# Three reorderings in a two-layer attention trunk: which queue issues the opening loads, when the memory rows are squared, when the block couples start

## The chip, the cores and the metric

The kernel runs on one core of a Trainium2 chip. The core has a matrix engine (TensorE, here PE, with its weight loader PEld), a vector engine (VectorE, DVE), a scalar engine (ScalarE, ACT), GpSimd (POOL) and SyncE (SP), which here only issues DMAs. Each engine works through its own instructions in order, and waits on semaphores for the others. The metric is the time of one execution in microseconds on the device.

## The reference, cut to what matters

Two layers over 256 tokens of width 1024, in fp32. Layer 0 has three head groups side by side: native sparse attention (compressed blocks, selected blocks, window), block attention (8 heads, which with 256 tokens and blocks of 256 is plain causal attention) and cross attention into 256 memory tokens. Layer 1 has retention and memory attention.

```python
def even_layer(x, mem_n, ...):
    h = rms_norm(x, norm_g)
    (nq, nkc, nvc, nks, nvs, nkw, nvw, ng, nz, mq, mk, mv, mz, eq, ez) = _split(h @ w_in, EVEN_SPLITS)
    kc = nsa_compress(rot(nkc), pe_k, w1_k, w2_k)
    vc = nsa_compress(heads(nvc), pe_v, w1_v, w2_v)
    gates = jax.nn.sigmoid(ng + gate_b).reshape(Bsz, T, NSA_BRANCHES, NSA_HEADS)
    a_out = nsa_attention(rot(nq), kc, vc, rot(nks), heads(nvs), rot(nkw), heads(nvw), gates)
    b_out = moba_attention(rot(mq), rot(mk), heads(mv))
    m_out = memory_attention(heads(eq), mem_n, w_mem_kv)
    y = jnp.concatenate([a_out * jax.nn.silu(nz), b_out * jax.nn.silu(mz),
                         m_out * jax.nn.silu(ez)], axis=-1) @ w_out
    return x + y
```

`mem_n` is the memory after an RMS norm over its rows, which needs the sum of squares of each row. `h` is the RMS norm of x, with the norm's weights folded into x's transposed tiles and the row scale applied later.

## The kernel before, in words

**Three products for one.** Each fp32 operand is split into a rounded part and a remainder (`whi` and `wlo` for weights, `xh` and `xl` for x), and `mm3` (lines 245 to 247) computes high times high, high times low and low times high. So each weight tile of 128 x 1024 (512 KB, a *unit* of two k-tiles by 512 columns) takes a load into a `raw` buffer, a cast on ScalarE into `whi` (`fetch`, line 166) and a subtraction on VectorE into `wlo` (`finish`, line 174). `unit()` hands out the next pair and fetches one that is used two units later. There are six `raw` buffers and four each of `whi` and `wlo`.

**The opening.** Before the stages, lines 380 to 398 issue the first loads by hand: x transposed (`xT`, eight k-tiles), the norm weights `g0`, and the weights of the first projection in halves and quarters. ScalarE issues x's k-tiles 0 and 1, SP the rest in order. PE runs a few warm-up matmuls (line 400), and then the first projection, k-tile by k-tile (lines 402 to 410): ScalarE multiplies x's k-tile by the norm weights into `xh` (`gain_cast`), VectorE makes `xl` (`gain_low`), and the k-tile's weights are split (`split`, lines 144 and 146). The weights of k-tile 0 are cast on VectorE, the others on ScalarE.

**Turns.** All that follows in layer 0 is a sequence of *stages*, each the projection of one group of columns, eight turns long: `compress`, `sparse_queries`, `sparse_gates`, `block_keys`, `block_queries`, `block_values`, `block_gates`, `memory_queries`, `memory_keys`, then the output projection `first_out`. A stage yields after each group of matmuls (twelve of 256 columns, or six of 512), and at each yield `drive` runs one `turn()`: it counts `slot[0]` up and advances every running *task* by one step. Tasks are generators; a step issues instructions on several engines and yields. The instructions go to each engine in exactly the order in which this program issues them (`manual_schedule`). Tasks in `first` (the attention couples) go before those in `active` (all else). The table `AT` names turns that tasks wait for with `until`.

**Couples.** `couple` computes attention for two pairs of heads, one step a turn: take four PSUM banks and issue the scores (step 0), maxima of the first pair (1), maxima of the second and exponentials of the first (2), exponentials of the second and softmax scaling of the first (3), scaling of the second (4), transposes of the first (5), copies of it and transposes of the second (6), copies (7), the product with the values in bank "o" (8); then `gated` multiplies with the gate path, casts, and subtracts (9 to 11), and the bank "o" is given back in step 9. Step 8 puts the couple's name into `made`, and a couple in `waiting` whose needs are all in `made` starts in that same turn. Four sparse couples, two block couples and the memory attention follow one another like this. `take(n, tags)` waits until n of the named banks are free; a bank given back in a turn is free in the next. `crowded` keeps "tr" from the couples, since the output projection accumulates there.

**Memory rows.** `memory_scale` loads the memory's rows (`memtok`), squares each of the two tiles on ScalarE with a row sum (`row_scale`, line 418), computes the reciprocal root on VectorE, and broadcasts it with two small matmuls into `rbm`, which `memory_keys` needs.

**Compression.** `compressed` waits for turn `AT["cmp"]`, rotates the keys (line 336 by way of `rotate`), copies the values (line 732), transposes three turns later (lines 739 and 740), adds the position weights from turn `AT["blk"]` on (line 759), and runs the compression matmuls in turn `AT["hid"]`, then the compressed scores.

Of the kernel before, what the change touches and what calls it, by code (L numbers as in the profile page):

```python
# [30 lines left out]
BANKS = {"pj": 3, "tr": 1, "t": 1, "s0": 1, "s1": 1, "o": 1}  # L31
FREE = ("s0", "s1", "t", "tr", "o")
NEG = -1e30
AT = {"rows": 4, "rows1": 4, "spread": 12, "ret": 75, "nsa": 12, "cmp": 15, "blk": 18, "hid": 24}
MAGIC = 12582912.0
PI_LO = 3.1415925
BASE = 16512 + 32 + 416 + 32
# [24 lines left out]
def trunk(  # L62
# [19 lines left out]
    nc = tc.nc  # L82
# [20 lines left out]
    def load(t, src):  # L103
        nc.sync.dma_start(t, src)
        return t
# [80 lines left out]
    waiting, first, active, made, slot, free = deque(), [], [], set(), [0], {}  # L186
# [16 lines left out]
    def take(n=1, tags=FREE[:4]):  # L203

        while sum(is_free(tag) for tag in tags) < n:
            yield
        got = [tag for tag in tags if is_free(tag)][:n]
        for tag in got:
            free[tag] = 1 << 30
        return got  # L210
# [6 lines left out]
    def drive(stage, every=1):  # L217

        for i, _ in enumerate(stage):
            if i % every == 0:  # L220
                turn()
# [6 lines left out]
    def pause(n):  # L228

        for _ in range(n):  # L230
            yield
# [6 lines left out]
    def making(task, *names):  # L238

        yield from task  # L240
        made.update(names)
# [121 lines left out]
    xraw, wraw = [], []  # L363
# [13 lines left out]
    order = ExitStack()  # L377
    order.enter_context(tc.manual_schedule(engines=MANUAL))
    g0 = vect[:, V_G0 : V_G0 + 8]
    load(wraw[0][:, 0:512], w512[2][:, 0:512])  # L380
    for kt in range(2):
        nc.scalar.dma_start(xraw[0][:, kt : kt + 1], xT[:, kt : kt + 1])
    load(g0, vec[:, V_G0 : V_G0 + 8])
    load(wraw[0][:, 512:1024], w512[2][:, 512:1024])
    for q in range(1, 4):
# [87 lines left out]
    def tables1():  # L473

        yield from until(AT["ret"])
        rows = load(cs[:, 64:].bitcast(I32), posrow.to_broadcast([P, T]))
# [4 lines left out]
    def norms():  # L481

        yield from until(AT["rows"])
        yield from row_scale(xrow, rstd0, D, AT["rows1"])
# [69 lines left out]
                else:  # L554
                    V.tensor_scalar(p[:, hh, a], p[:, hh, a], sm[:, hh, tok : tok + 1], None, op0=ALU.mult)  # L555

    def couple(jobs, causal, products, close, name, need=None):

        spans, cols, blocks = (SPAN, 384, range(3)) if causal else (HALF, 512, (0, 2, 1, 3))
        tags = yield from take(4, FREE)  # L560
        ss, todo = [], []
        for i, (q, k, gate) in enumerate(jobs):
            ss.append([bank(tag) for tag in tags[2 * i : 2 * i + 2]])
            for tok, a in enumerate(spans):
                for hh in range(2):
                    rows = slice(64 * hh, 64 * hh + 64)
                    todo.append((ss[i][hh][:, a], q[rows, tok * P : (tok + 1) * P], k[rows, : a.stop - a.start], True, True))
        side_by_side(todo)
        yield
        ps, ms, ns, pts = [[None] * 2 for _ in range(4)]  # L570

        def maxima(i):

            ps[i] = tl("p", [P, 2, 512], 2)
            ms[i] = tl("mx", [P, 2, 2], 4)
            ns[i] = tl("sm", [P, 2, 2], 4)
            for hh in range(2):
                if causal:
                    for tok, a in enumerate(spans):
                        V.tensor_tensor_reduce(ps[i][:, hh, a], ss[i][hh][:, a],  # L580
                                               cpak[:, C_CAUSAL + a.start : C_CAUSAL + a.stop], -1.0, 3e38,
                                               ALU.add, ALU.min, ms[i][:, hh, tok : tok + 1])
                else:
                    V.tensor_reduce(ms[i][:, hh], ss[i][hh].rearrange("p (a k) -> p a k", a=2), AX.X, ALU.max, negate=True)
            if causal:
                give(*tags[2 * i : 2 * i + 2])

        def exponentials(i):

            for hh in range(2):  # L590
                for tok, a in enumerate(spans):
                    src = ps[i][:, hh, a] if causal else ss[i][hh][:, a]
                    S.activation(ps[i][:, hh, a], src, AF.Exp, bias=ms[i][:, hh, tok : tok + 1],  # L593
                                 scale=-1.0 if causal else 1.0, accum_out=ns[i][:, hh, tok : tok + 1])
            if not causal:
                give(*tags[2 * i : 2 * i + 2])

        def scale(i):

            softmax_scale(ps[i], ns[i], spans, jobs[i][2], 0 if jobs[i][2] is None and causal else 3)  # L600

        def turned(i):

            held = yield from take(2, FREE)
            return [(tag, transposes([ps[i][:, hh, b * P : (b + 1) * P] for b in blocks], tag)) for hh, tag in enumerate(held)]

        def copies(i, held):

            pts[i] = tl("pt", [P, 2, 512], 2)
            for hh, (tag, b) in enumerate(held):  # L610
                got = S.copy(pts[i][:, hh, :cols], b)
                give(tag)
            return got

        maxima(0)
        yield
        maxima(1)
        exponentials(0)
        yield
        while need is not None and "gates" not in made:  # L620
            yield
        exponentials(1)
        scale(0)
        yield
        scale(1)
        yield
        first = yield from turned(0)
        yield
        copies(0, first)
        second = yield from turned(1)  # L630
        yield
        got = copies(1, second)
        yield
        while need is not None and need not in made:
            yield
        tag, = yield from take(1, ("o",))
        o = bank(tag)
        side_by_side(products(o, pts), got)
        made.add(name)
        yield  # L640
        yield from close(o)
# [6 lines left out]
    def gated(o, szT, y, kts):  # L648

        n = (kts.stop - kts.start) * T  # L650
        yf = tl("tmp2", [P, 512], 3)[:, :n].rearrange("p (k t) -> p k t", t=T)
        V.tensor_tensor(yf, o[:, :n].rearrange("p (k t) -> p k t", t=T), szT[:, kts], ALU.mult)
        give("o")
        yield
        S.copy(y[:, 0, kts], yf)
        yield
        V.tensor_tensor(y[:, 1, kts], yf, y[:, 0, kts].bitcast(F32), ALU.subtract)
# [185 lines left out]
    def memory_queries():  # L843
        nonlocal eqT, szm
        ps_e = yield from project_turned((xh, xl))
        eqT = tl("s2", [P, 2, T], NS)
        szm = tl("s2", [P, 2, T], NS)

        def post():
            scaled(ps_e[0], rb0, 0.125, eqT)  # L850
            yield from gate_path(ps_e[1:], rb0, szm)

        active.append(making(post(), "eqT", "szm"))
# [14 lines left out]
    def memory_scale():  # L868
        nonlocal rstdm, rbm
        mrow = [load(tl("raw", [P, 1024], NRAW), memtok[:, tok]) for tok in range(2)]  # L870
        rstdm = tl("rstdm", [P, 2])
        yield
        yield from row_scale(mrow, rstdm, D)
        yield
        rbm = tl("rbm", [P, T])
        tag, = yield from take()
        b = bank(tag)
        for tok in range(2):
            PE.matmul(b[:, tok * P : (tok + 1) * P], rstdm[:, tok : tok + 1].to_broadcast([P, P]), ident, start=True, stop=True)
        yield  # L880
        V.tensor_copy(rbm, b[:, :T])
        give(tag)

    def memory_keys():
        nonlocal memk, memv
        assert {"mh", "rbm"} <= made
        ps = yield from project_mem((mh, ml))
        memk = tl("s2", [P, 2, T], NS)
        memv = tl("s2", [P, 2, T], NS)

        def post():
            mem_keys(ps, rstdm, rbm, memk, memv)
            yield

        active.append(making(post(), "memk"))
# [31 lines left out]
    def block_couple(c):  # L927
        nonlocal yb
        if c == 0:
            yb = tl("y", [P, 2, 4, T], 2, F32R)  # L930

        def products(o, pts):
            todo = []
            for i in range(2):
                todo += causal_products(o[:, i * T : i * T + T], pts[i],
                                        lambda hh, kt: mvt[:, kt, (4 * c + 2 * i + hh) * 64 : (4 * c + 2 * i + hh) * 64 + 64],
                                        True, True)
            return todo

        yield from couple([(mq[:, 2 * c + i], mk[:, 2 * c + i], None) for i in range(2)], True, products,  # L940
                          lambda o: making(gated(o, szb, yb, slice(2 * c, 2 * c + 2)), f"Yb{c}"), f"yb{c}")

    def memory_keys1():
        nonlocal k1, v1m
# [31 lines left out]
    drive(block_values())  # L976
    active.append(making(memory_scale(), "rbm"))
    drive(block_gates())
    waiting.extend(({"mq", "mk", "mvt", "szb", f"yb{c - 1}" if c else "yn3"}, block_couple(c)) for c in range(2))
    drive(memory_queries())  # L980
    crowded = True
    drive(memory_keys())


    def part(acc, tok, c0, n, y, k, wh, wl, start, stop):
# [321 lines left out]
```

## Time and profile before

| | us |
|---|---|
| median of 3 runs | 427.76 |
| lowest, highest | 427.15, 428.31 |
| the profiled execution | 427.74 |
| its span, first to last instruction | 425.9 |
| mean granted TensorE clock | 0.999 |
| DMA: 74.23 MB over the span | mean 174 GB/s |

A row of the timeline gives start and length in us, engine, line, operation, and output and inputs by tile name; in brackets the idle time of the engine before it and what ended that. Neighbouring instructions of a kind are merged, with their count behind an x. PE's lengths are modelled and overlap, so the distance from start to start tells more than the length does.

### The profile page before, as it was taken

The page shows a single profiled execution, that of the slowest core. Times are in us where ns is not written, and L with a number is a line of the kernel's source. Part 1 is how long each engine was busy: PE and PEld are TensorE (multiplying, and loading weights), DVE is VectorE, ACT ScalarE, POOL GpSimd, SP SyncE. Part 2 cuts the span into 40 slices and gives each one's busy share as a digit, 9 for nine tenths or more (in the row PEclk, how much of TensorE's full clock was granted, in tenths as well). Part 3 has the DMA queues.
Part 4 walks back from the last instruction along what each step waited for, and adds up shares of the span by engine and source line. Part 5 has one row for each costly group of instructions (what it writes and reads, how often), then busy time and mean ns, then how long its engine had stood idle before and what let it go on. Part 6 is the DMA issues. An engine that isn't in the chain of part 4 may idle for free.

```text
span 425.9 us, 7020 instructions
## 1 busy us (share of the span) xinstructions
PE 417.7 (98%) x2620; PEld 361.4 (85%) x2620; DVE 305.7 (72%) x675; ACT 245.6 (58%) x453; POOL 1.9 (0%) x9
## 2 busy tenths in 40 slices
PE   8999999999999999999999999999999999999994
PEld 6889987878889887779999988889998888888884
DVE  3878996977678577588578675677887467685545
ACT  4768476777777586755456344456444445545613
POOL 1000000000000000000000000000000000000000
PEclk9999999999999999999999999999999999999999
DMA  7997545254563852536445545546444555656202
GB/s 247 334 372 254 194 136 192 67 184 160 184 191 110 287 175 97 169 128 195 157 145 168 170 167 168 196 159 198 158 158 159 184 192 175 205 170 189 80 0 99
DMA packets 22801, 74.23 MB, mean 174 GB/s; under 512 B 2928, under 2 KB 4464, under 8 KB 22768
## 3 DMA queue, kind: packets, MB, share of 16 engines
q1 hardware_dynamic: 22192, 73.14, 52.2%
q10 hardware_dynamic: 576, 0.66, 0.6%
q8 instruction: 20, 0.33, 0.3%
q14 instruction: 13, 0.11, 0.1%
HBM read 72.73 MB, written 1.05 MB: 173 GB/s over the span
## 4 chain that ended last, share of the span: by engine, by line
PE 92%; DVE 3%; DMA 3%; ACT 1%; issue 0%; SPq 0%; DVEq 0%; ACTq 0%
PE pj L245 23%; PE pj L247 22%; PE pj L246 22%; PE o L116 3%; PE s L409 2%; PE s L324 2%; PE s L116 2%; PE t L324 1%; DMA raw<-in_w 1%; PE tr L245 1%; PE tr L247 1%; PE tr L246 1%; DMA raw<-in_memtok 1%; PE t L116 1%; PE s L246 1%; PE s L247 1%
## 5 line engine op out<-in xcount | busy, mean ns | idle before, releaser
L174 DVE TENSOR_TENSOR wlo<-raw,whi 128x1024 fp32r<-128x1024 f32 (+1 forms) x118 | 142.1, 1207 | 61.8 <-ACT whi L166 59.7
L166 ACT CAST whi<-raw 128x1024 fp32r<-128x1024 f32 (+1 forms) x118 | 121.7, 1036 | 88.4 <-PE pj L247 38.0
L245 PE MATMUL pj<-whi,big 128*128 128x512 f32 (+2 forms) x256 | 97.3, 383 | 0.0
L246 PE MATMUL pj<-wlo,big 128*128 128x512 f32 (+2 forms) x256 | 96.1, 376 | 0.0
L247 PE MATMUL pj<-whi,big 128*128 128x512 f32 (+2 forms) x256 | 95.8, 374 | 0.0
L245 PE MATMUL pj<-big,whi 128*128 128x256 f32 x256 | 73.6, 287 | 0.0
L247 PE MATMUL pj<-big,wlo 128*128 128x256 f32 x256 | 72.6, 284 | 0.0
L246 PE MATMUL pj<-big,whi 128*128 128x256 f32 x256 | 72.5, 283 | 0.0
L245 PEld LDWEIGHTS pj<-whi,big 128*128 128x128 f32 x256 | 48.2, 188 | 9.3 <-issue 1.5
L247 PEld LDWEIGHTS pj<-whi,big 128*128 128x128 f32 x256 | 48.2, 188 | 8.7
L246 PEld LDWEIGHTS pj<-wlo,big 128*128 128x128 f32 x256 | 48.3, 189 | 8.1 <-DVE wlo L174 0.4
L245 PEld LDWEIGHTS pj<-big,whi 128*128 128x128 f32 x256 | 49.0, 191 | 1.9 <-issue 1.8
L246 PEld LDWEIGHTS pj<-big,whi 128*128 128x128 f32 x256 | 49.0, 192 | 0.1
L247 PEld LDWEIGHTS pj<-big,wlo 128*128 128x128 f32 x256 | 49.0, 191 | 0.0
L593 ACT ACTIVATE p<-p,mx 128x128 f32<-128x128 f32 (+1 forms) x48 | 21.2, 443 | 5.3 <-DVE mx L580 5.3
L245 PE MATMUL pj<-whi,y 128*128 128x512 f32 x42 | 16.9, 407 | 0.0
L247 PE MATMUL pj<-whi,y 128*128 128x512 f32 x42 | 16.4, 390 | 0.0
L246 PE MATMUL pj<-wlo,y 128*128 128x512 f32 x42 | 16.3, 391 | 0.0
L555 DVE TENSOR_SCALAR p<-p,sm 128x256 f32<-128x256 f32 (+1 forms) x48 | 12.7, 322 | 0.6
L343 ACT ACTIVATE big<-raw,vec 128x256 fp32r<-128x256 f32 x16 | 7.7, 505 | 5.2 <-DMA vec<-in_vec 2.5
L553 ACT ACTIVATE p<-p,sm 128x256 f32<-128x256 f32 (+1 forms) x16 | 7.6, 484 | 4.9 <-DVE sm L549 4.0
L580 DVE CUSTOM_DVE_ANT_0 p<-s,cst 128x128 f32<-128x128 f32 (+1 forms) x24 | 7.1, 355 | 4.4 <-PE s L116 4.3
(349 smaller groups left out, 644.5 us busy)
## 6 DMA issues: line engine op xcount, KB each, us to landing
raw<-in_w SPq DMA_DIRECT2D x90, 512.0 KB, 3.9
raw<-in_wout SPq DMA_DIRECT2D x28, 512.0 KB, 4.1
v<-in_xtok SPq DMA_DIRECT2D x4, 512.0 KB, 6.4
raw<-in_w SPq DMA_DIRECT2D x4, 280.0 KB, 5.3
raw<-in_w SPq DMA_DIRECT2D x4, 256.0 KB, 6.2
v<-in_w SPq DMA_DIRECT2D x2, 512.0 KB, 7.5
raw<-in_memT SPq DMA_DIRECT2D x2, 512.0 KB, 4.2
raw<-in_memtok SPq DMA_DIRECT2D x2, 512.0 KB, 4.9
```

Source lines behind the costliest of these rows:

```text
L116: ins = PE.matmul(out, lhs, rhs, start=start, stop=stop)
L166: S.copy(hi, raw)
L174: V.tensor_tensor(lo, raw, hi.bitcast(F32), ALU.subtract)
L245: PE.matmul(ps, lh, rh, start=start, stop=False, skip_group_check=shared)
L246: PE.matmul(ps, lh, rl, start=False, stop=False, skip_group_check=shared)
L247: return PE.matmul(ps, ll, rh, start=False, stop=stop, skip_group_check=shared)
L324: PE.transpose(b[:, i * P : (i + 1) * P], a, ident)
L343: S.activation(hi[:, kt], raw[:, kt - k0], AF.Copy, scale=g[:, kt : kt + 1])
L409: PE.matmul(ps_k[tok], x[:, kt, tok * P : (tok + 1) * P], w, start=kt == 0 and i == 0, stop=kt == KT - 1 and i == 2)
L553: S.activation(p[:, hh, a], p[:, hh, a], AF.Copy, scale=sm[:, hh, tok : tok + 1])
L555: V.tensor_scalar(p[:, hh, a], p[:, hh, a], sm[:, hh, tok : tok + 1], None, op0=ALU.mult)
L593: S.activation(ps[i][:, hh, a], src, AF.Exp, bias=ms[i][:, hh, tok : tok + 1], scale=-1.0 if causal else 1.0, accum_out=ns[i][:, hh, tok : ...
```

## The change

It makes five small edits and adds and removes no computation. The first load on SP is x's k-tile 0, in front of the norm weights; the first half of the weights and x's k-tile 1 are issued by ScalarE. `cmp` and `hid` move by one turn. `memory_scale` waits one turn more before the squares and two more before the broadcast. The block couples no longer need `szb`, the gate path's tile (it is read in step 9), and the second one takes its banks in the order "tr", "s0", "s1", "t". `crowded` is set after `memory_keys` instead of before.

```diff
-AT = {"rows": 4, "rows1": 4, "spread": 12, "ret": 75, "nsa": 12, "cmp": 15, "blk": 18, "hid": 24}
+AT = {"rows": 4, "rows1": 4, "spread": 12, "ret": 75, "nsa": 12, "cmp": 14, "blk": 18, "hid": 23}
...
-    load(wraw[0][:, 0:512], w512[2][:, 0:512])
-    for kt in range(2):
-        nc.scalar.dma_start(xraw[0][:, kt : kt + 1], xT[:, kt : kt + 1])
+    nc.scalar.dma_start(wraw[0][:, 0:512], w512[2][:, 0:512])
+    nc.scalar.dma_start(xraw[0][:, 1:2], xT[:, 1:2])
+    load(xraw[0][:, 0:1], xT[:, 0:1])
     load(g0, vec[:, V_G0 : V_G0 + 8])
...
-    def couple(jobs, causal, products, close, name, need=None):
+    def couple(jobs, causal, products, close, name, need=None, banks=FREE):
...
-        tags = yield from take(4, FREE)
+        tags = yield from take(4, banks)
...
-        yield
+        yield from pause(2)
         yield from row_scale(mrow, rstdm, D)
-        yield
+        yield from pause(3)
...
-                          lambda o: making(gated(o, szb, yb, slice(2 * c, 2 * c + 2)), f"Yb{c}"), f"yb{c}")
+                          lambda o: making(gated(o, szb, yb, slice(2 * c, 2 * c + 2)), f"Yb{c}"), f"yb{c}",
+                          banks=("tr", "s0", "s1", "t") if c else FREE)
...
-    waiting.extend(({"mq", "mk", "mvt", "szb", f"yb{c - 1}" if c else "yn3"}, block_couple(c)) for c in range(2))
+    waiting.extend(({"mq", "mk", "mvt", f"yb{c - 1}" if c else "yn3"}, block_couple(c)) for c in range(2))
     drive(memory_queries())
+    drive(memory_keys())
     crowded = True
-    drive(memory_keys())
```

## The prediction, made before the changed kernel was run

> **What bounds the kernel now.** I read the page first, then the waits of PE and of its weight loader, then the timelines of PE, ScalarE and VectorE wherever PE waited.
>
> ```profile
> span 425.9 us, 7020 instructions
> PE 417.7 (98%) x2620; PEld 361.4 (85%) x2620; DVE 305.7 (72%) x675; ACT 245.6 (58%) x453; POOL 1.9 (0%) x9
> PE s L324 <- DVE p L555: 1.2, 1, 1.2
> ```
>
> TensorE is the bound: matmuls stand back to back for 98% of the span. No instruction is added or removed by this change (loads swap queues, tasks swap turns), so all it can win is time in which PE waits. After the opening there are only two such places: 1.2 us for the scaled softmax `p` of a couple, and a small one for `ym`, shown further down. I add PE's lead-in, and the cost of PE switching between full matmuls and the side-by-side 64-row ones.
>
> The larger wait, on PE, with the same transposes of a later couple as a yardstick:
>
> ```profile
> 110.22 0.28 PE L245 MATMUL pj<-big,whi 128*128 128x256 f32 x1
> 111.66 0.28 PE L245 MATMUL pj<-big,whi 128*128 128x256 f32 x1
> 115.86 0.28 PE L247 MATMUL pj<-big,wlo 128*128 128x256 f32 x1
> 117.29 1.03 PE L324 MATMUL s<-cst,p 128*128 128x128 f32 x6 [1.16 <-DVE p L555]
> 136.11 0.82 PE L324 MATMUL s<-cst,p 128*128 128x128 f32 x6
> ```
>
> A turn's group of twelve matmuls takes 111.66 - 110.22 = 1.44 us, 0.12 each. So PE was free at 115.86 + 0.12 = 115.98 and began at 117.29: **1.31 us** lost. The six transposes then took 1.03 instead of 0.82, as half of them still waited: **0.21 us**.
>
> Why was `p` late?
>
> ```profile
> 103.60 0.49 ACT L611 COPY pt<-o 128x384 f32<-128x384 f32 x1
> 107.71 1.06 ACT L418 ACTIVATE raw<-raw 128x1024 f32<-128x1024 f32 x1 [3.62 <-DMA raw<-in_memtok]
> 108.77 1.03 ACT L166 CAST whi<-raw 128x1024 fp32r<-128x1024 f32 x1
> 109.70 1.05 ACT L418 ACTIVATE raw<-raw 128x1024 f32<-128x1024 f32 x1
> 110.76 1.03 ACT L166 CAST whi<-raw 128x1024 fp32r<-128x1024 f32 x1
> 112.00 0.40 ACT L593 ACTIVATE p<-p,mx 128x128 f32<-128x128 f32 x1
> 115.10 0.50 ACT L593 ACTIVATE p<-p,mx 128x256 f32<-128x256 f32 x1
> 117.01 0.51 ACT L553 ACTIVATE p<-p,sm 128x256 f32<-128x256 f32 x1 [1.32 <-DVE sm L549]
> 109.83 1.23 DVE L174 TENSOR_TENSOR wlo<-raw,whi 128x1024 fp32r<-128x1024 f32 x1 [5.49 <-ACT whi L166]
> 116.95 0.74 DVE L555 TENSOR_SCALAR p<-p,sm 128x128 f32<-128x128 f32 x3
> ```
>
> ScalarE runs in order. The first memory square (L418) stood ahead of a weight cast (L166) and waited 3.62 us for its rows; the cast could have gone at 104.1. VectorE's `wlo` needs that cast, so VectorE idled 5.49 us, then worked off its queue and reached the scaling of `p` at 116.95.
>
> **The change part by part.**
>
> *Memory squares.* Turn N is the one at 105.29. Rows are still asked for at turn N-2; the squares move from N-1 and N to N and N+1. The cast of N's unit is issued before turn N, so it now runs at 104.1 to 105.1 and its `wlo` until 106.4, 4.7 us sooner than 111.1. Queued behind the waiting square are now the second square, the next cast and the exponentials. Bounding pessimistically, I let the second square start no earlier than its 109.70: cast at 110.76 and exponentials from 112.00 to 115.6 as before. What changes is VectorE: output product, both maxima and the first rsqrt step fit before 112.9, the next `wlo` before 114.1, the first scaling after the fourth exponential (113.8) by 115.2. ScalarE's share of it (L553, 0.51) follows the last exponential: 116.2. PE's first three transposes need only VectorE's share (115.2, against 115.98); the fourth needs 116.2 at 116.3. Cover: 0.8 and 0.1 us; with the second square at its data, 0.5. I take the whole **1.52 us**. Bounds: 0 and 1.52. The later broadcast of the memory scale finds its banks taken at turn N+8 and goes at N+10, its copy at N+11, still before the memory keys (N+14).
>
> *Block scores.* Without `szb` the first block couple starts in the turn of the last sparse product instead of one later. With "tr" in place of "o" (which the product holds) the second starts in the first one's product turn instead of two later; moving `crowded` is what lets it have "tr". So couples run 1, 3 and 3 turns earlier (block 0, block 1, memory). PE's work is the same, but products and scores now stand together:
>
> ```profile
> 105.29 1.52 PE L116 MATMUL o<-pt,s 128*64 128x256 f32 x16
> 107.17 0.93 PE L116 MATMUL s<-s,v 64*128 64x128 f32 x8
> 123.79 1.52 PE L116 MATMUL o<-pt,s 128*64 128x256 f32 x16
> 125.67 0.38 PE L245 MATMUL pj<-big,whi 128*128 128x256 f32 x1
> 127.30 0.93 PE L116 MATMUL s<-v,v 64*128 64x128 f32 x8
> ```
>
> Joined, product to scores is 107.17 - 105.29 = 1.88 us, the same as product to full matmul when apart (125.67 - 123.79). But the group standing between the two takes 127.30 - 125.67 = 1.63 instead of 1.44. Joining saves that 0.19 once per block couple: **0.38 us** (bounds 0 and 0.4).
>
> *Memory attention, three turns earlier,* leaves the out-projection's last group of `ym` nothing to wait for:
>
> ```profile
> 183.84 0.40 PE L246 MATMUL pj<-wlo,ym 128*128 128x512 f32 x1
> 184.23 0.50 PE L247 MATMUL pj<-whi,ym 128*128 128x512 f32 x1
> 184.56 0.40 PE L245 MATMUL pj<-whi,ym 128*128 128x512 f32 x1
> 184.80 0.40 PE L246 MATMUL pj<-wlo,ym 128*128 128x512 f32 x1
> ```
>
> The first two stand 0.39 apart, the last two 0.24; the third matmul needs the `ym` remainder that VectorE has just written. I take 0.39 - 0.23 = **0.16 us** (bounds 0 and 0.16).
>
> *`cmp` 15 to 14, `hid` 24 to 23.* PE does not wait here now, so nothing can be won directly; the question is cover.
>
> ```profile
> 33.55 1.06 ACT L166 CAST whi<-raw 128x1024 fp32r<-128x1024 f32 x1
> 35.73 0.37 ACT L732 ACTIVATE tmp<-t,rstd 128x128 f32<-128x128 f32 x1 [0.50 <-DVE gates L728]
> 35.61 1.21 DVE L174 TENSOR_TENSOR wlo<-raw,whi 128x1024 fp32r<-128x1024 f32 x1
> 38.10 0.69 DVE L336 TENSOR_TENSOR rot_a<-pj,ctq 128x512 f32<-128x512 f32 x1 [1.27 <-PE o L739]
> ```
>
> The compress copies (L732) now stand ahead of a weight cast on ScalarE: it starts at 36.1 instead of 33.55, its `wlo` ends at 38.4 instead of 36.8. L739 is PE's work of turn 18 and ended VectorE's wait at 38.10; this unit is used in turn 19, a group of 1.44 later, about 39.5, so some 1.1 us of cover stay. In exchange the 1.27 us that VectorE waited for L739 go, as those transposes come a turn earlier; VectorE ends within 0.3 us of where it was. The compressed scores stay in their turn: the first sparse couple holds the banks. Price 0; if the cover were gone, up to the 2.55 us by which the cast moves.
>
> *The opening.* SP's first issue becomes x's k-tile 0 (128 KB) instead of half a weight tile (256 KB); that half goes out on ScalarE's queue ahead of k-tile 1. The norm weights keep their place behind it.
>
> ```profile
> 5.65 1.04 ACT L343 ACTIVATE big<-raw,vec 128x256 fp32r<-128x256 f32 x2 [2.50 <-DMA vec<-in_vec]
> 7.50 0.62 ACT L144 CAST whi<-raw 128x512 fp32r<-128x512 f32 x1 [0.80 <-DMA raw<-in_w]
> 8.43 0.51 ACT L343 ACTIVATE big<-raw,vec 128x256 fp32r<-128x256 f32 x1 [0.31 <-DMA raw<-in_xT]
> 9.06 0.62 ACT L144 CAST whi<-raw 128x512 fp32r<-128x512 f32 x1
> 8.17 1.21 PE L409 MATMUL s<-whi,big 128*128 128x512 f32 x4
> 9.74 1.20 PE L409 MATMUL s<-whi,big 128*128 128x512 f32 x4
> ```
>
> The first cast waits for the norm weights (5.65), and they may land some tenths sooner. But PE's second and third k-tiles start at 8.17 and 9.74, right behind the casts of weights that land near 7.5 and 9.0. Before the second half lands, the same 772 KB must have come over both queues as before. What is won on k-tile 0 therefore turns into a longer wait at 8.17: price **0**. From outside: 256 KB of the stream land in about 8.43 - 7.50 = 0.93 us, so the 128 KB that change queues are worth 0.47 us either way. The Trainium skill ("DMA: Bandwidth & Descriptors", section "Issuing engines are not separate DMA queues") says that DMAs issued by different engines run on the same 16 DMA engines and interleave, and that issuing from several saves only issue time. By that rule the opening is worth nothing; by queues of their own it would be worth the 0.47. No row here decides it.
>
> **Sum.** 1.52 + 0.38 + 0.16 + 0 = 2.06 us off the profiled execution's 427.74 (span 425.9 and 1.84 around it): 425.7. That execution is 0.02 from the median of the runs, 427.76.
>
> **The rivals.**
> - *Queues of their own:* everything behind SP's first load lands 0.47 sooner: 425.2. For it: only the second half's place in SP's queue; against it: the later waits (8.43) show a stream that is full.
> - *More sharing:* ScalarE's queue carries 128 KB more ahead of the second half, which lands 0.47 later: 426.1.
> - *The square still blocks:* moved by one turn it holds the next cast and the exponentials instead, the cover of 0.1 us is gone, and the stall stays: 425.7 + 1.52 = 427.2. For it: exponentials from 112.00 as before in my pessimistic bound; against it: VectorE's 5.49 idle us are gone.
> - *VectorE becomes the bound (slower):* block 1's maxima and scaling now fall into the turns of block 0's output steps.
>
> ```profile
> L580 DVE CUSTOM_DVE_ANT_0 p<-s,cst 128x128 f32<-128x128 f32 (+1 forms) x24 | 7.1, 355 | 4.4 <-PE s L116 4.3
> L555 DVE TENSOR_SCALAR p<-p,sm 128x256 f32<-128x256 f32 (+1 forms) x48 | 12.7, 322 | 0.6
> 102.00:104.00 2.00, 2.00 (x19) 2.00 (x18) 2.00 (x3) 2.00 (x5) 0.00 (x0) 1.00 0.71 188
> ```
>
> Eight maxima at 0.355 and six scalings at 0.322 are 4.8 us. With two and a half `wlo` of 1.23 and about 1 us of output steps that is an estimated 8.9 us in five turns, which PE fills for 5 x 1.44 + 1.88 + about 1.5 = 10.6. It decides if VectorE enters them more than 1.7 us behind; each further us then delays a `wlo` and PE. With all 4.8 exposed: 430.5. Against it: sparse couples stack the same way, and at 102 to 104 VectorE is full (2.00) while PE is too.
>
> **How the numbers follow.** Forecast 0.55 (425.2 to 426.4), own queues 0.12, more sharing 0.11, square still blocks 0.15, VectorE bound 0.07. About 0.3%, here 1.28 us, is what a measurement can tell from no change: the edges are 426.5 and 429.0. Faster: 0.51 of the forecast's 0.55, 0.12 and 0.08 of the sharing case make 0.71. Same: the remaining 0.07 and the 0.15 make 0.22. Slower: 0.07. The range reaches from the own-queue case with a little for error, 425.0, to the blocked square, 427.3, and leaves out the slower case and tails.
>
> **What would show it.** Right: no PE wait for L555 near 114 to 118; a weight cast on ScalarE between the L611 copies and the first L418; scores directly behind the product, without `pj` between, for both block couples; `ym` matmuls evenly 0.23 apart; k-tile 1 still near 8.2. Wrong: a PE wait for `wlo` or `whi` near 39 to 50 (cover at `cmp` gone) or between the block couples; k-tile 1 at 7.7 or 8.6; a wait of the exponentials that still ends at 117.

## The result, and the profile after

| | before | after |
|---|---|---|
| median in us | 427.76 (427.00 to 428.85, 5 runs) | 425.46 (424.62 to 425.79, 5 runs) |
| ratio to before | | 0.9942, 95% interval 0.9923 to 0.9962 |
| span of the profiled execution | 425.9 | 423.9 |
| the changed kernel timed once more, later | 427.97 (10 runs) | 425.90 (6 runs), ratio 0.9951, 0.9936 to 0.9966 |

The change makes the kernel 2.3 us faster, 2.1 us in the second timing. The prediction was 425.7, in a range from 425.0 to 427.3. One execution of a kernel further down, e_norms, ran at a granted clock of 0.558 and took 694.15 us; it was the profiled one, and it is left out of all times and of the table of starts.

The same lines of the page as before the change (busy time, share of the span and instructions of each engine), now of the changed kernel:

```profile
span 423.9 us, 7022 instructions
PE 416.1 (98%) x2620; PEld 361.4 (85%) x2620; DVE 306.1 (72%) x675; ACT 246.0 (58%) x453; POOL 1.9 (0%) x9
```

And PE's waits in it (what it wrote, which engine and line ended the wait, then us in total, times, and the longest):

```profile
PE t L400 <- POOL kcbd L716: 1.3, 1, 1.3
PE s L409 <- ACT whi L144: 0.3, 1, 0.3
PE pj L246 <- DVE wlo L174: 0.3, 1, 0.3
```

The wait of 1.2 us for `p` has left the list. What remains is the lead-in (L400), which before had too, and two waits of 0.3 in the first 28 us, which before's profile did not have.

The place of the old stall, in the timelines of ScalarE, VectorE and PE of the changed kernel (start, length, engine, line, operation, output and inputs, and in brackets the idle time ahead with what ended it):

```profile
105.04 1.07 ACT L166 CAST whi<-raw 128x1024 fp32r<-128x1024 f32 x1
108.27 1.06 ACT L418 ACTIVATE raw<-raw 128x1024 f32<-128x1024 f32 x1 [2.17 <-DMA raw<-in_memtok]
106.14 1.23 DVE L174 TENSOR_TENSOR wlo<-raw,whi 128x1024 fp32r<-128x1024 f32 x1 [1.37 <-ACT whi L166]
114.41 0.74 DVE L555 TENSOR_SCALAR p<-p,sm 128x128 f32<-128x128 f32 x3
116.78 0.82 PE L324 MATMUL s<-cst,p 128*128 128x128 f32 x6
```

The cast stands ahead of the square now, so `wlo` follows at 106.14, where before it began at 109.83. ScalarE still waits 2.17 us for the memory's rows, and the next cast and the exponentials stand behind, but they are still in time for PE. VectorE scales `p` at 114.41 instead of 116.95, PE takes up the transposes at 116.78 without a wait, and the six take 0.82 us.

The product of the last sparse couple and the scores of the first block couple, then `ym` in the output projection, both on PE:

```profile
122.49 1.52 PE L116 MATMUL o<-pt,s 128*64 128x256 f32 x16
124.37 0.93 PE L116 MATMUL s<-v,v 64*128 64x128 f32 x8
125.88 0.39 PE L245 MATMUL pj<-big,whi 128*128 128x256 f32 x1
181.88 0.39 PE L245 MATMUL pj<-whi,ym 128*128 128x512 f32 x1
182.10 0.39 PE L246 MATMUL pj<-wlo,ym 128*128 128x512 f32 x1
182.33 0.39 PE L247 MATMUL pj<-whi,ym 128*128 128x512 f32 x1
182.56 0.39 PE L245 MATMUL pj<-whi,ym 128*128 128x512 f32 x1
```

Product to scores is 1.88 us and scores to the next projection matmul 1.51 us, each as it was before when they stood apart (127.30 to 128.81 for the latter, by the matmul that stands at 128.81 in before's timeline). Gone is the group that lay between them, at 1.63 instead of 1.44. From the first to the fourth `ym` matmul it takes 0.68 us; in before it took 184.56 - 183.50 = 1.06.

### The profile page after: what moved, and what is told of

Its sections match the earlier page's. It is cut to its first block, busy times and chain, and to the rows that moved or that the text cites. A ratio compares the mean times of both kernels' runs of the same rounds, so it can differ in the third digit from the quotient of the medians.

```text
span 423.9 us, 7022 instructions
## 1 busy us (share of the span) xinstructions
PE 416.1 (98%) x2620; PEld 361.4 (85%) x2620; DVE 306.1 (72%) x675; ACT 246.0 (58%) x453; POOL 1.9 (0%) x9
## 4 chain that ended last, share of the span: by engine, by line
PE 84%; DMA 6%; DVE 4%; ACT 3%; issue 1%; SPq 0%; DVEq 0%; ACTq 0%
PE pj L245 22%; PE pj L246 21%; PE pj L247 21%; PE o L116 3%; DMA raw<-in_w 2%; DMA raw<-in_memT 2%; DMA v<-in_xtok 2%; PE s L324 2%; PE s L116 1%; PE t L324 1%; PE tr L245 1%; PE tr L246 1%; PE tr L247 1%; DVE wlo L174 1%; PE s L245 1%
## 5 line engine op out<-in xcount | busy, mean ns | idle before, releaser
L116 PE MATMUL o<-pt,s 128*64 128x256 f32 (+1 forms) x96 | 10.0, 350 | 0.0
L553 ACT ACTIVATE p<-p,sm 128x256 f32<-128x256 f32 (+1 forms) x16 | 7.7, 484 | 3.8 <-DVE sm L549 2.3
```

What stands on the lines that cost most here:

```text
L116: ins = PE.matmul(out, lhs, rhs, start=start, stop=stop)
L553: S.activation(p[:, hh, a], p[:, hh, a], AF.Copy, scale=sm[:, hh, tok : tok + 1])
```

## The experiments

Every kernel issues the same matmuls in nearly the same order, so PE's timelines can be laid side by side. One matmul marks the border between the opening and the rest: the `wlo` product that stands at 57.02 in before. Behind it lies all that the squares, the couples and `ym` do; ahead of it lie the opening and `cmp` and `hid`.

The border in PE's timeline of before:

```profile
57.02 0.39 PE L246 MATMUL pj<-wlo,big 128*128 128x512 f32 x1
```

and in that of the changed kernel:

```profile
57.47 0.39 PE L246 MATMUL pj<-wlo,big 128*128 128x512 f32 x1
```

In the table the third to fifth columns are the starts of the first matmuls of k-tiles 1 and 4 and of the border matmul in each kernel's profile, the sixth is the span less the fifth, and the last is the ratio of the timed runs to before's in the same set of runs.

| kernel | opening | k-tile 1 | k-tile 4 | border | border to end | ratio, 95% interval |
|---|---|---|---|---|---|---|
| before | old | 8.17 | 12.59 | 57.02 | 368.92 | 1 |
| the change | new | 8.42 | 12.64 | 57.47 | 366.42 | 0.9942 (0.9923 to 0.9962) |
| again | new | 8.33 | 12.59 | 57.85 | 366.04 | 0.9951 (0.9936 to 0.9966) |
| e_opening | new | 8.42 | 12.74 | 57.53 | 369.35 | 1.0001 (0.9981 to 1.0022) |
| e_turns | old | 8.83 | 13.06 | 57.53 | 368.84 | 0.9999 (0.9979 to 1.0020) |
| e_pauses | old | 8.72 | 12.85 | 57.09 | 368.33 | 0.9974 (0.9961 to 0.9987) |
| e_couples | old | 8.65 | 13.10 | 57.30 | 369.68 | 0.9973 (0.9953 to 0.9993) |
| e_squares | old | 8.93 | 13.14 | 57.47 | 367.27 | 0.9964 (0.9946 to 0.9982) |
| e_pauses_szb | old | 8.76 | 12.86 | 57.59 | 366.67 | 0.9944 (0.9926 to 0.9963) |
| e_core | old | 8.91 | 13.18 | 57.73 | 366.07 | 0.9942 (0.9919 to 0.9964) |
| e_rows | new | 8.17 | 12.57 | 58.08 | 366.43 | 0.9953 (0.9935 to 0.9971) |
| e_norms | new |  | | | | 0.9937 (0.9922 to 0.9952) |
| e_norms_old | old | 8.78 | 13.00 | 57.03 | 366.04 | 0.9930 (0.9918 to 0.9943) |
| e_norms_b | new | 8.85 | 12.93 | 56.98 | 366.04 | 0.9928 (0.9904 to 0.9951) |

### One part of the change at a time

**e_opening**: the three opening lines alone.

```diff
-    load(wraw[0][:, 0:512], w512[2][:, 0:512])
-    for kt in range(2):
-        nc.scalar.dma_start(xraw[0][:, kt : kt + 1], xT[:, kt : kt + 1])
+    nc.scalar.dma_start(wraw[0][:, 0:512], w512[2][:, 0:512])
+    nc.scalar.dma_start(xraw[0][:, 1:2], xT[:, 1:2])
+    load(xraw[0][:, 0:1], xT[:, 0:1])
```

> The kernel before with the reordered opening loads alone. If both queues share the same stream, k-tile 0 starts up to 0.3 us sooner, k-tile 1 at 8.2 to 8.5 as in the whole change, and the span changes by less than 0.3 us, or rises by up to 0.5 if the 0.5 us that the whole change is behind at 28 us come from the opening. If the queues were their own, k-tile 1 starts near 7.7 and the span falls by about 0.5.

Median 428.77 beside 428.54 for before. The interval reaches 0.2% to either side, which is 0.9 us, so a difference of 0.5 us would not show. K-tile 1 stands at 8.42, within 8.2 to 8.5; k-tile 0 starts at 6.69, not sooner than before's 6.37. **e_turns**: the two turns alone.

```diff
-... "cmp": 15, "blk": 18, "hid": 24 ...
+... "cmp": 14, "blk": 18, "hid": 23 ...
```

> The kernel before with cmp 14 and hid 23 alone. If the cover holds as worked out, PE has no wait between 33 and 57 us, the span changes by less than 0.2 us, and VectorE's wait of 1.3 us for L739 is replaced by one of about 1.4 us for the later weight cast. If the cover is gone, a PE wait for wlo of 0.5 to 2.5 us stands between 38 and 50 us.

Median 428.37 beside 428.54, with an interval as wide. PE waits nowhere between 33 and 57 us, and VectorE waits 1.37 us for the later cast, as expected. What the two parts are worth by themselves, if anything, is too small for these times.

**e_pauses**: the two pauses of `memory_scale` alone.

```diff
-        yield
+        yield from pause(2)
         yield from row_scale(mrow, rstdm, D)
-        yield
+        yield from pause(3)
```

> The kernel before with the two longer pauses in memory_scale alone. If the gain sits where PE waited for the scaled p, the 1.3 us wait near 117 us is gone and the span falls by 1.3 to 1.6 us, about 1.5, with nothing changed elsewhere but the place of the two broadcast matmuls. If the square only blocks the next cast and the exponentials instead, a PE wait of 0.5 to 1.3 us for L555 or L553 stays near 117 us and the span falls by 0 to 0.8.

Median 427.60 beside 428.54: 0.9 us, where the stall alone is 1.5. That is neither of the two cases expected: the wait near 117 is gone, and PE loses elsewhere. PE's waits in its profile show why:

```profile
PE pj L245 <- ACT ym L655: 1.4, 1, 1.4
```

and PE's timeline of the same kernel shows where it comes from:

```profile
121.77 1.52 PE L116 MATMUL o<-pt,s 128*64 128x256 f32 x16
123.65 0.71 PE L879 MATMUL s<-cst,rstdm 128*128 128x128 f32 x4
127.15 0.93 PE L116 MATMUL s<-v,v 64*128 64x128 f32 x8
179.62 1.95 PE L116 MATMUL o<-pt,s 128*64 128x256 f32 x16
183.01 0.50 PE L245 MATMUL pj<-whi,ym 128*128 128x512 f32 x1 [1.44 <-ACT ym L655]
```

The wait for `p` is gone, and one of 1.44 us for `ym` has come. The later broadcast of the memory scale (L879) now takes a PSUM bank in just the turn in which the first block couple wants four. Of the five named banks the product still holds "o" and the broadcast has one more. So the couple finds only three, starts two groups after the product instead of one, and everything behind it is a turn late. The last product of the memory attention (179.62) then has no projection group between it and `ym`, so nothing covers the gate path whose cast on ScalarE (L655) PE waits for.

**e_couples**: the block couples' part alone (no `szb`, the banks' order, `crowded` later).

```diff
-        tags = yield from take(4, FREE)
+        tags = yield from take(4, banks)
...
+                          banks=("tr", "s0", "s1", "t") if c else FREE)
...
-    waiting.extend(({"mq", "mk", "mvt", "szb", f"yb{c - 1}" if c else "yn3"}, block_couple(c)) for c in range(2))
+    waiting.extend(({"mq", "mk", "mvt", f"yb{c - 1}" if c else "yn3"}, block_couple(c)) for c in range(2))
     drive(memory_queries())
-    crowded = True
     drive(memory_keys())
+    crowded = True
```

> The kernel before with the edits on the couples alone (no szb in the needs, the banks of the second block couple, crowded set later). If joined products and scores save their switches and the memory attention comes earlier, the span falls by about 0.8 us (0.4 for two joins, 0.4 for the ym group of the out-projection), and the wait near 117 us stays at 1.3. If VectorE becomes the bound between the block couples, PE waits for wlo there and the span rises.

Median 427.37 beside 428.54: 1.2 us, more than the 0.8 expected. The memory attention's transposes, which e_core is about to show, are 0.22 of it (1.25 us in before, 1.03 here, at 171.56). The stall for `p` is still there (1.5 us in its profile), and PE waits for no `wlo`. Its profile is long because of what followed that stall; that is told at the end.

### The parts put together

**e_squares** moves the squares but not the distance to the broadcast. It tests the bank story: the same earlier PE, but a broadcast that collides with nobody.

```diff
-        yield
+        yield from pause(2)
         yield from row_scale(mrow, rstdm, D)
         yield
```

> Only the memory squares move, by one turn; the broadcast of the memory scale keeps its distance behind them. Theory (the pauses alone lost part of their gain because the later broadcast took a PSUM bank in the turn in which the first block couple wanted four, which put all later couples one turn back and left no projection group between the memory attention's product and ym): here the broadcast goes one group after the transposes and the couples stand as before, so the wait for p at 117 (1.3 us) and the stretched transposes (0.2) go and no wait for ym appears: 1.5 us under the kernel before (1.2 to 1.8), span about 424.4. Rival (PE that comes 1.5 us sooner always uncovers the tail of the memory attention): the wait for ym of 1.4 is there again, and the time is 0.1 to 1.1 us under the kernel before.

PE's timeline of e_squares:

```profile
120.61 0.60 PE L879 MATMUL s<-cst,rstdm 128*128 128x128 f32 x4
122.58 1.52 PE L116 MATMUL o<-pt,s 128*64 128x256 f32 x16
182.30 0.50 PE L245 MATMUL pj<-whi,ym 128*128 128x512 f32 x1
```

The broadcast goes ahead of the product, the couples stand as before, `ym` waits for nothing, and the time is 426.64 beside 428.26: 1.6 us. The rival, that an earlier PE always uncovers the tail, falls. From the border on the profile is 368.92 - 367.27 = 1.65 us shorter: 1.52 for the stall, and 0.13 for a broadcast that no longer stands between the two pairs of transposes. By the starts on either side it cost PE 0.59 us there (120.18 - 117.29 = 2.89 in before, less the 0.21 of stretched transposes, beside 118.52 - 116.43 = 2.09 in e_squares) and costs 0.45 in its new place (122.58 - 118.85 = 3.73 beside 123.79 - 120.51 = 3.28 in before).

**e_pauses_szb** is e_pauses without `szb` among the block couples' needs.

> Both pauses, and the block couples without szb among their needs; the banks as before. Theory: the first block couple now starts in the product's own turn, ahead of the broadcast, so nothing takes its banks; the product and scores of block 0 stand together (0.19), block 1 and the memory attention start one turn sooner than in the kernel before, so ym's group of matmuls is evenly spaced (0.38): 1.52 + 0.19 + 0.38 = 2.1 us under the kernel before (1.8 to 2.4), no wait for ym. Rival (the wait for ym of the pauses alone is a matter of VectorE and ScalarE being late, and needs all three turns): a wait for ym of over 0.5 stays, and the time is about 1.2 us under the kernel before.

426.13 beside 428.26: 2.1 us, no wait for `ym`. The couple that starts in the product's own turn is ahead of the broadcast and has its banks first. From the border on it gains 0.60 over e_squares: the first join (0.19) and the even `ym` group (0.38) are 0.57, less 0.08 for the memory attention's transposes, which take 1.33 us here and 1.25 in e_squares. Some 0.1 us is left that I cannot place.

**e_core** is the change without the opening and without `cmp` and `hid`.

> The change without the new opening and without cmp and hid. Theory (both are worth nothing): like the changed kernel, 2.1 to 2.6 us under the kernel before; first k-tile 1 matmul at 8.2 to 8.4, no wait of PE between 33 and 57. Rival (the opening lands the norm weights sooner, or the earlier transposes free VectorE): 0.4 us or more of the gain is missing, so 2.0 us or less under the kernel before.

425.66 beside 428.26: 2.6 us, and a ratio of 0.9942, which is that of the whole change. So what the opening and the two turns add is again too small for these times, and from the border on the changed kernel in again is the same within 0.03 (366.04 and 366.07). From the border on e_core gains another 0.60 over e_pauses_szb. The second join is 0.19 of it. From block 0's product to the first projection matmul behind block 1's scores, PE's timeline of e_pauses_szb shows:

```profile
139.09 1.52 PE L116 MATMUL o<-pt,v 128*64 128x256 f32 x16
145.12 0.39 PE L245 MATMUL pj<-big,whi 128*128 128x256 f32 x1
```

and that of e_core:

```profile
139.23 1.52 PE L116 MATMUL o<-pt,v 128*64 128x256 f32 x16
142.19 0.39 PE L245 MATMUL pj<-big,whi 128*128 128x256 f32 x1
```

The first takes 6.03 us with two projection groups of 1.44 between, the second 2.96 with none: 6.03 - 2.88 - 2.96 = 0.19. Another part is in the transposes of the memory attention, here in PE's timeline of e_pauses_szb:

```profile
171.23 1.33 PE L324 MATMUL s<-cst,p 128*128 128x128 f32 x8
```

and in that of e_core:

```profile
168.37 1.04 PE L324 MATMUL s<-cst,p 128*128 128x128 f32 x8
```

The same eight transposes take 1.33 us and, two turns earlier, 1.04: some of them waited for their half of the scaled `p`. In e_pauses_szb the sixth starts at 172.01, right behind ScalarE's scaling (L553), which runs from 171.44 to 171.96. That is 0.29. Again some 0.1 us is left.

### A loss in the profile after, and a failed cure

In the changed kernel's profile PE stumbles once behind the border: one matmul comes 0.39 after its predecessor instead of 0.12. Its rows on ScalarE and PE:

```profile
95.97 0.91 ACT L343 ACTIVATE big<-raw,vec 128x256 fp32r<-128x256 f32 x2 [2.09 <-DMA raw<-in_memT]
103.72 0.69 ACT L922 ACTIVATE v<-pj,rstd 128x512 f32<-128x512 f32 x1
104.08 0.28 PE L247 MATMUL pj<-big,wlo 128*128 128x256 f32 x1
104.47 0.39 PE L245 MATMUL pj<-big,whi 128*128 128x256 f32 x1
```

ScalarE stood 2.09 us behind the memory's transposed rows, came late to L922, and PE needed the bank that L922 reads. **e_rows** lets ScalarE multiply those rows one turn later.

```diff
             mraw = load(tl("raw", [P, 1024], NRAW), memT[:, 4 * q : 4 * q + 4].rearrange("p k t -> p (k t)")).rearrange("p (k t) -> p k t", k=4)
-            yield
+            yield from pause(2)
```

> The whole change, and the memory's transposed rows are multiplied by the norm weights one turn later than in it. Theory (the new loss of the changed kernel at 104.5, 0.28 us, comes from ScalarE standing 2.1 us behind the load of those rows, with the copy that PE needs queued behind it): the wait of ScalarE for in_memT falls under 0.7, PE's wait for L922 is gone, and the time is 0.2 to 0.3 us under the changed kernel, 2.4 to 2.9 under the kernel before. Rival (ScalarE is short of time there whatever stands first): PE's wait near 104 stays at 0.2 to 0.3 and the time is that of the changed kernel; or the later rows make memory_keys wait, which shows as a wait of PE for big after 130 and a time over that of the changed kernel.

Ratio 0.9953, not better than the change. ScalarE's wait for the rows is gone, but PE's of 0.3 us is not, as the rival said; VectorE and PE of e_rows:

```profile
102.71 1.67 DVE L347 SCALAR_TENSOR_TENSOR big<-raw,vec,big 128x256 fp32r<-128x256 f32 x4
104.29 0.75 DVE L921 TENSOR_SCALAR v<-pj,rstd 128x512 f32<-128x512 f32 x1
105.09 0.38 PE L245 MATMUL pj<-big,whi 128*128 128x256 f32 x1
```

Both halves of the remainders (L347) now fall together on VectorE, 1.67 us ahead of L921, the other reader of the values' banks. PE starts 0.05 us after L921 ends. The wait has only changed engines. In **again**, the changed kernel profiled once more, ScalarE waited 1.22 us for the rows and PE lost nothing there, as in before (1.45), e_core (1.26) and the others: in these profiles it goes with when a load lands, and it costs 366.42 - 366.04 = 0.38 us when that is late.

### The first 28 us

Whatever a kernel gained or lost behind the border, the border itself wandered from 57.02 to 58.08. The first profiles suggested that the new opening was sooner at k-tile 4 and gave that back at 28 us. Three kernels were to tell: **again** (the changed kernel unaltered), **e_norms** (the changed kernel with `rows1` at 5, which puts three small steps of the reciprocal root behind a `wlo` instead of ahead of it), and **e_norms_old** (e_norms with the old opening).

```diff
-AT = {"rows": 4, "rows1": 4, "spread": 12, ...
+AT = {"rows": 4, "rows1": 5, "spread": 12, ...
```

> The changed kernel itself, once more, beside the next two. Over the profiles so far the first matmul of k-tile 4 stood at 12.57 to 12.74 with the new opening (three profiles) and at 12.59 to 13.18 with the old one (seven). Theory (the new opening is worth some 0.3 us there, and PE gives it back at 27.9, where it waits for a wlo): k-tile 4 at 12.5 to 12.8, a wait of PE for wlo of 0.2 to 0.9 near 28. Rival (the landings scatter, whatever the order): k-tile 4 anywhere from 12.6 to 13.2.

> The changed kernel with rows1 at 5: the first three small steps of the reciprocal root (0.58 us of VectorE) that stand ahead of the wlo for which PE waits at 27.9 go behind it. Theory: that wlo starts as soon as its cast is done or 0.5 us earlier, PE's wait of 0.3 there is gone, and the time is 0.2 to 0.4 us under the changed kernel. Rival (the weights' landing sets that wlo): the wait stays, since the cast is what ends VectorE's idle time before the wlo, and the time is the changed kernel's within 0.15.

> The same with the old opening. Theory: k-tile 4 about 0.3 us later (12.9 to 13.2), no wait of PE at 28, so 0.2 to 0.4 us over the kernel with the new opening; the opening would then be worth something once the wait behind it is gone. Rival (scatter): no difference beyond 0.15 us in time, and k-tile 4 within the range of the new opening.

In this set of runs before took 427.97, again 425.90, e_norms 425.35 and e_norms_old 424.94. As e_norms left no profile to lay beside the others, the same kernel ran once more, on another chip, as **e_norms_b**.

> rows1 at 5 with the new opening once more, for a profile at full clock. With the old opening this edit gave 424.94, with the new one 425.38, though k-tile 4 stood 0.3 to 0.4 us sooner in every profile with the new opening. Theory (the lead of the new opening is lost where PE is fed by the stream of weights): k-tile 4 at 12.5 to 12.8, and then a wait of PE for wlo near 28 of 0.2 us or more, whose cast was itself waiting for its load; by 30.6 PE stands no sooner than with the old opening (30.59). Rival (the opening is lost nowhere, the two times differ by scatter): no wait near 28, PE's matmul of 30.59 stands at 30.2 to 30.3, and the span is 0.3 us shorter than with the old opening (423.1).

424.94 beside 428.31 for before on that chip. The timelines of ScalarE and VectorE in again, around the `wlo` for which PE waited 0.8 us at 28.29:

```profile
25.25 1.05 ACT L166 CAST whi<-raw 128x1024 fp32r<-128x1024 f32 x1 [0.35 <-DMA raw<-in_w]
26.52 0.16 DVE L137 SCALAR_TENSOR_TENSOR rstd<-rs_t,rstd 128x2 f32<-128x2 f32 x1
27.01 1.23 DVE L174 TENSOR_TENSOR wlo<-raw,whi 128x1024 fp32r<-128x1024 f32 x1 [0.34 <-issue]
```

and those of ScalarE, VectorE and PE in e_norms_b:

```profile
25.02 1.05 ACT L166 CAST whi<-raw 128x1024 fp32r<-128x1024 f32 x1 [0.38 <-DMA raw<-in_w]
25.68 0.16 DVE L137 SCALAR_TENSOR_TENSOR rstd<-rs_t,rstd 128x2 f32<-128x2 f32 x1
26.11 1.22 DVE L174 TENSOR_TENSOR wlo<-raw,whi 128x1024 fp32r<-128x1024 f32 x1 [0.27 <-ACT whi L166]
27.55 0.40 PE L246 MATMUL pj<-wlo,big 128*128 128x512 f32 x1
```

In again the cast was done at 26.3, but VectorE still had small steps of the root to issue, and `wlo` began at 27.01. In e_norms_b the cast is done at 26.07, `wlo` follows at once, and PE doesn't wait. In e_norms_old `wlo` starts at 26.11 as well. The border stands at 57.0 in both, whichever opening they have. So of the 0.9 us by which `wlo` is sooner, 0.7 is VectorE's queue and 0.2 is the cast, which waits for its load in both kernels. The rival about the weights' landing does not explain this wait, but the landing has a share in others: in e_rows, where PE waits longest at this place (0.95 us), the cast itself ended only at 26.88.

My theory of the opening got the signs in again right: k-tile 4 at 12.59, and a wait of 0.8 near 28. It failed on the kernels that were to test it. The old opening should have cost 0.2 to 0.4 us beside the new one, and was 0.4 faster. e_norms_b has the new opening and reached k-tile 4 at 12.93, outside the range that I gave; its `wlo` made PE wait nowhere. The ratios are 0.9937 and 0.9928 with the new opening and 0.9930 with the old one, so a difference between the openings can't be told from scatter here.

With `rows1` at 5 the kernel is faster than the changed kernel in the same set of runs: by 0.55 us with the new opening, where the runs still overlap (424.81 to 425.62 beside 425.32 to 426.06), and by 0.96 with the old one, where they don't (424.68 to 425.07). The gain lies ahead of the border, since from there to the end e_norms_old and again take 366.04 both.

## Why the prediction was right

**The stall, 1.52 predicted.** 1.65 in e_squares, where it is nearly alone, with 0.13 of that for the broadcast. Mechanism and size hold. The pessimistic bound was close to what came: the exponentials start at 112.11 (bound 112.00) in the changed kernel, no sooner than in before, and still `p` is scaled 2.5 us sooner. So VectorE's queue had decided, not ScalarE's.

**The pauses are not safe by themselves.** I had looked at where the later broadcast finds a bank in the whole change, and there it is harmless. I had not said that it depends on the removal of `szb`. Alone, the same edit gives back 1.44 us at `ym`. The sum holds because one part shields another.

**The joins, 0.38 predicted.** The scores stand behind the product in both block couples. The first is 0.19 of e_pauses_szb's 0.60, the second 0.19 of e_core's 0.60.

**`ym`, 0.16 predicted: mis-sized.** It is 1.06 - 0.68 = 0.38. I took one spacing of 0.39 as the wait and the 0.34 and 0.33 beside it as the normal start of a group; at 0.23 apiece in the changed kernel, all three were waiting.

**Two terms that I missed.** One is the memory attention's transposes. In PE's timeline of before:

```profile
173.90 1.25 PE L324 MATMUL s<-cst,p 128*128 128x128 f32 x8
```

and of the changed kernel:

```profile
168.47 1.03 PE L324 MATMUL s<-cst,p 128*128 128x128 f32 x8
```

These 0.22 us could have been read from before, though PE's waits did not list them. The other is 0.13 for the place of the broadcast.

**`cmp` and `hid`, 0 predicted.** As described: VectorE's 1.27 us for L739 became 1.37 us for the cast, and PE did not wait.

```profile
36.42 1.04 ACT L166 CAST whi<-raw 128x1024 fp32r<-128x1024 f32 x1
37.49 1.23 DVE L174 TENSOR_TENSOR wlo<-raw,whi 128x1024 fp32r<-128x1024 f32 x1 [1.37 <-ACT whi L166]
```

**The opening, 0 predicted: not told apart from its rivals.** e_opening and e_core agree with 0, but their intervals of 0.9 us to either side leave room for the 0.47 of both rivals (425.2 by own queues, 426.1 by more sharing). The Trainium skill ("DMA: Bandwidth & Descriptors", section "Issuing engines are not separate DMA queues") states that loads issued by several engines share the same DMA engines; no run here shows it or speaks against it. K-tile 1 "near 8.2" was more exact than the chip is: with the old opening it stood between 8.17 and 8.93 (eight profiles, mean 8.72), with the new one between 8.17 and 8.85 (five, mean 8.44). Before's own 8.17 is the early end. At k-tile 4 the means are 12.97 and 12.69, and at the border, with `rows1` at 4, 57.39 (seven) and 57.73 (four). The ranges overlap each time, so whether the new opening is a little sooner at first and loses that by 57 us stays open. One reading was not exact either: the cast at 9.06, which I put down to weights that land near 9.0, has no wait of its own; it stood behind the multiplication at 8.43, which waited for x.

**The sum.** Behind the border the change is worth 368.92 - 366.04 = 2.88 us where no load is late, not 2.06. Of that 1.52 + 0.13 + 0.38 + 0.38 + 0.22 = 2.63 are placed and 0.25 are not. In the profile after it is 2.50, as 0.38 went at 104.47. Ahead of the border that profile is 0.45 behind before's, which had the earliest border of all kernels with `rows1` at 4. 2.50 - 0.45 = 2.05 is what the spans show, and it meets 2.06 by luck: the part behind the border was underrated by 0.8, and the border, priced at 0, wandered by 1.1 us from one kernel to the next. VectorE did not become the bound: behind the border the changed kernel's PE waits for no `wlo`.

## What to carry to other kernels

When a task is moved, ask which shared thing it now takes in which turn, not only which engine it occupies: here one PSUM bank, taken a turn too late, cost as much as the stall that the move removed. Small stretched spacings in a group of matmuls (0.33 instead of 0.23) can be waits too, and they are missing from a list of waits; compare a group with an undisturbed one of the same shape. And before a change in the first microseconds is judged by one profile, profile the same kernel twice: here the same opening scattered by 0.8 us.

## What the runs showed of the hardware that was not expected

The clock can fall after one stall of 1.5 us in the midst of dense work. In e_couples, behind the wait of 1.54 us for `p` that ended at 117.96, the windows view shows the granted clock (the number ahead of the last two; the first is the stretch's length) at 0.55 for 119 to 122, and 1.00 on either side:

```profile
114.00:118.00 4.00, 2.46 (x22) 2.25 (x20) 3.83 (x19) 2.68 (x12) 0.00 (x0) 1.00 0.58 196
119.00:122.00 3.00, 3.00 (x16) 3.00 (x17) 2.92 (x7) 2.33 (x5) 0.00 (x0) 0.55 0.22 85
123.00:127.00 4.00, 4.00 (x39) 3.65 (x38) 3.67 (x5) 3.77 (x6) 0.00 (x0) 1.00 0.55 202
```

Its matmuls of 128x256 then come 0.21 us apart instead of 0.12, so a group of twelve takes about 2.6 us instead of 1.44. In single microseconds the clock is 0.64 for 119 to 120, 0.50 for 121 to 122 and 0.65 for 122 to 123; by these shares it stood at one half from about 119.3 to 122.7, an estimated 3.4 us. e_opening waited 1.59 us at the same place, and its clock stayed at 1.00. The Trainium skill ("TensorE: Matmul & The Clock Gate", section "Part 1: The HAM clock gate (the "warmup" mystery)") describes a free-running window of about 3.4 us after which an idle array drops to half its clock. The trace agrees with it in the half and in the length, and a free-running window would fit a drop that comes in some executions only; but here the array had been idle for 1.54 us, less than half a window.

The mean granted clock of the timed runs, on record for all but the first few of before, tells how often this happens. Of the kernels that keep the stall at 117 (before, e_opening, e_turns, e_couples), 20 of 121 runs have a mean clock of 0.995 or less. Of the kernels without it none of 82 has, and e_pauses with its wait of 1.44 us for `ym` is among them. A clock of one half for 3.4 of 427 us lowers the mean by an estimated 0.004, which is the step seen: 0.993 to 0.995 in those runs, 0.996 to 0.999 in all others. They are the long runs too (before 431.08 with a median of 428.54; e_opening 431.23 with 428.77): their medians are 1.6 to 2.2 us above those of the other runs of the same kernel in the same set. When the clock fell in them was seen in the one profile of e_couples and is not shown for the rest. If it is the same drop, the stall of 1.3 us also costs some 2 us in one run of six, which a median hides.
